# Split weights at a pitch of 130 words per stationary tile, and pairs of activations at multiples of 64 bytes

## The chip, the cores and the metric

The kernel runs on one core of one Trainium2 chip. The metric is the device time of one execution in microseconds (us); three runs of the kernel before took 2317.48 to 2319.41 us, median 2319.04. Five engines work side by side: the tensor engine (PE in the profile; PEld is its loading of stationary operands), the vector engine (DVE), the scalar engine (ACT), GpSimd (POOL), and the sync engine (SP), which issues the loads from DRAM. Matmuls read a stationary operand and a moving one from SBUF, a memory of 128 partitions, and write to PSUM.

## The reference

Three transformer blocks of width 1024 are applied one after the other to 512 tokens, in float32. Nearly all of the arithmetic is products of an activation with a weight matrix; between them stand norms, gates and mixers.

```python
# block 1: adaptive norm; dilated attention and an HGRN2 recurrence; gated sum
proj = h @ w_in[l]
y = sigmoid(g_a) * (o_a @ w_branch_a[l]) + sigmoid(g_b) * (o_b @ w_branch_b[l])
x = x + gate[:, None] * (y @ w_out[l])
...
# block 2: latent attention and a long convolution; a gated feed forward with a short convolution
x = x + y_mix @ w_out[i]
up = _dwconv3(h @ w_up[i], ffn_conv_w[i], ffn_conv_b[i])
x = x + (jax.nn.silu(g) * u) @ w_down[i]
...
# block 3: mLSTM, SSD and retention; a gated feed forward; a last norm
```

## The kernel before

**Products.** Activations lie transposed, with 128 features on the partitions and the 512 tokens along a row. Each operand of these products is split into two float32r parts, a high one and a low one, whose sum is the number. A product of one stationary tile (128 by 128) with one activation tile (128 by 512) is then three matmuls: high weight by high activation, low weight by high activation, high weight by low activation. `acc_T` (line 119) issues them for `nk` tiles in a row into one PSUM bank; eight tiles, 24 matmuls, make one output tile of `proj_T` (line 129). So a new stationary operand is loaded ahead of every matmul.

**Weights.** `raw` (line 95) loads a group of up to 1024 words per partition from DRAM by the sync engine's queue into one of `WRAW` = 4 buffers `wr`. `parts` (line 106) makes the high part `wh` on the scalar engine (line 110, a copy that casts) and the low part `wl` on the vector engine (line 111, a subtraction; four of 370 on GpSimd), in one of `WHL` = 3 buffers each. A buffer of `wh` holds eight stationary tiles end to end, tile k at word 128 k, that is at 512 k bytes. `proj_N` (line 137) uses the same groups the other way round: there an activation tile is stationary and 256 columns of the weights move. The inverse transform of the long convolution (line 1387) and the shared rotary key (line 1241) do so too.

**Activations.** `pair` (line 162) allocates the two parts of an activation tile: `A0` to `A7` live all through, others (`B`, `C`, `a`, `oa`, `ob`, `y` and so on) in pools that open and close with the stages. Where a pair lies depends on what its pool holds before it: the pools stack up, so that a small tile of 160 bytes per partition (`lb`, line 634) or of 16 bytes (`pss`, line 1259) shifts all that is allocated above it.

**Order.** The order of instructions on each engine is settled when the program is built; at run time semaphores alone decide when one may start. A group of weights may be split once the matmuls that read its buffer three groups earlier are done.

Of the kernel before, what the change touches and what calls it, by code (L numbers as in the profile page):

```python
# [25 lines left out]
# ---------------------------------------------------------------- host layout  # L26
def tiles_T(w, ksplit):
    """(K, N) -> for each k split [N/128, 128, nk*128]; lhsT tiles of 128 columns."""
    K, N = w.shape
    a = w.reshape(K // P, P, N // P, P).transpose(2, 1, 0, 3)  # L30
    out, k0 = [], 0
    for nk in ksplit:
        out.append(np.ascontiguousarray(a[:, :, k0 : k0 + nk]).reshape(N // P, P, nk * P))
        k0 += nk
    return out


def tiles_N(w, nk, gc):
    """(K, N) -> [N/gc, K/(128 nk), 128, nk*gc]; moving groups of gc columns."""
    K, N = w.shape  # L40
    a = w.reshape(K // (P * nk), nk, P, N // gc, gc).transpose(3, 0, 2, 1, 4)
    return np.ascontiguousarray(a).reshape(N // gc, K // (P * nk), P, nk * gc)


def cols(v):
    """A vector of n*128 features -> [128, n]."""
    return np.ascontiguousarray(np.asarray(v).reshape(-1, P).T)


def pad_rows(v):  # L50
    """A [k<=128, n] block -> [128, n] with zero rows below."""
    v = np.asarray(v)
    o = np.zeros((P, v.shape[1]), v.dtype)
    o[: v.shape[0]] = v
    return o


class K:
    """The engines, the pools and the operations that all blocks share."""
# [34 lines left out]
    # -------------------------------------------------------------- weights  # L94
# [7 lines left out]
    def w(self, src, n=1024, eng=None):  # L102
        """One group of weights from DRAM, split exactly into two float32r parts."""
        return self.parts(self.raw(src, n), n, eng)

    def parts(self, r, n=1024, eng=None):
        nc = self.nc
        hi = self.wp.tile([P, 1024], F32R, tag="whi", bufs=self.WHL, name=self.name("wh"))
        lo = self.wp.tile([P, 1024], F32R, tag="wlo", bufs=self.WHL, name=self.name("wl"))
        nc.scalar.copy(out=hi[:, :n], in_=r[:, :n])  # L110
        (eng or nc.vector).tensor_tensor(out=lo[:, :n], in0=r[:, :n], in1=hi[:, :n].bitcast(F32), op=ALU.subtract)  # L111
        return hi, lo

    # -------------------------------------------------------------- products
# [3 lines left out]
    def acc_T(self, ps, w, act, nk, start=True, stop=True, m=P, n=T, k0=0):  # L118
        """ps[m, n] += w^T act over nk tiles of 128, three passes each."""
        hi, lo = w  # L120
        for k in range(nk):
            ah, al = act[k0 + k]
            wh, wl = hi[:, k * P : k * P + m], lo[:, k * P : k * P + m]
# [4 lines left out]
    def proj_T(self, srcs, act, tag="mm", bufs=3, nks=(8,), eng=None):  # L128
        """One tile [128 features, 512 tokens] of act @ w; srcs are the k groups."""
# [7 lines left out]
    def proj_N(self, grp, act, nk, gc, evac, tag="mm", bufs=3):  # L137
        """[512 tokens, gc features] of act @ w; grp is [ksplits, 128, nk*gc]."""
# [3 lines left out]
        ws = [self.w(grp[s], nk * gc) for s in range(nks)]  # L142
# [14 lines left out]
    def last_pe(self):  # L157
        """The last instruction of the tensor engine so far."""
        return next(i for i in reversed(self.nc.cur_bb.bb.instructions) if i.engine == mybir.EngineType.PE)

    # -------------------------------------------------------------- pairs
# [3 lines left out]
    def A(self, i):  # L165
        """The i-th of eight pairs that live all through."""
        return self.pair(self.hp, f"A{i}")

    def split(self, pr, src, lo="v", p=P):
        """Two float32r parts of an SBUF tile (or, with lo on the vector engine, a PSUM tile)."""  # L170
# [7 lines left out]
    def split_scaled(self, pr, src, g, p=P):  # L178
        """The parts of src * g with g per partition."""
# [8 lines left out]
    # -------------------------------------------------------------- norms  # L188
    def sq_add(self, acc, i, x, scale=None, tag="sq"):
        """acc (+)= (x * scale)^2 for tile i of a sum; returns acc."""  # L190
# [11 lines left out]
    def col_sums(self, acc, tag="t", bufs=2):  # L202
        """Sums over the partitions of acc [128, 512] (or of several), as [128 tokens, 4]."""
# [13 lines left out]
    def rsqrt(self, src, n, inv, eps=EPS):  # L217
        """(src * inv + eps) ** -0.5 for a small [128, n]."""
# [6 lines left out]
    def rows(self, r, sb=True, tag="t", bufs=2):  # L225
        """r [128 tokens, 4] as rows over all partitions, [128, 512] (in SBUF or PSUM)."""
# [16 lines left out]
class HeadRows:  # L243
    """Factors per token of two heads as rows over 64 partitions each."""

    def __init__(self, k, pool, bufs=1):
        nc = k.nc
        self.k, self.n = k, 0
        # the two parts of the rows (from 0 and from 32), and what spreads them
# [8 lines left out]
    def __call__(self, r, out):  # L258
        """r [128 tokens, 4, 2] -> out [128, 512]."""
# [14 lines left out]
class Norm:  # L274
    """A norm whose factor per token is applied to the products: pairs of x * g are ready tile by tile."""
# [10 lines left out]
    def finish(self):  # L286
        """The pairs; the factor per token follows when it is first used."""
        return self.pairs
# [24 lines left out]
def consts1():  # L313
    v = np.arange(TAB)
    dist = 127 - v + 384  # table entry v holds distance (p - u + 384) with v = u - p + 127
# [48 lines left out]
def rel_table(k, pool):  # L364
    """rel_bias plus the multiplicity of each distance (a last row), as a table in DRAM."""
# [15 lines left out]
def skew_rows(k, s1, s2, pr):  # L381
    """The rows of the table of two heads, once per partition."""
# [3 lines left out]
class Ada:  # L386
    """One third of silu(c) @ w_ada as columns [128, 8], in two halves; with `row`, the second one as a row by the tensor engine."""
# [47 lines left out]
def start(k, early):  # L435
    """x -> the pairs of h, with the work that needs no activations between the loads."""
    nc = k.nc
    with k.tc.tile_pool(name="b1s", bufs=1) as pool:
# [7 lines left out]
        # partly in the places of the pairs of h  # L446
# [53 lines left out]
def attn1(k, h, tab, oa, op):  # L500
    """The merged dilated attention; appends the gated pairs of o_a. Returns the columns of the gate."""
    nc = k.nc
    with k.tc.tile_pool(name="a1", bufs=1) as p:
# [3 lines left out]
        def proj(pr):  # L507
            ps = k.proj_T([k.aps["w1q"][pr]], h)
            # the two parts of a head over each other, k's first part twice
# [119 lines left out]
def bounds(k, p):  # L629
    """What the lower bounds of the forget gates make of tanh."""  # L630
    nc = k.nc
    # lower bound: softmax over the two rows, first of the cumulated
    l0, l1 = k.v("lb0", 0, 8), k.v("lb1", 0, 8)
    lb = p.tile([P, 8, 5], F32, tag="lb", name="lb")
# [8 lines left out]
    # fs = (1 - lb) / 2, fb = lb + fs  # L643
# [3 lines left out]
    # k / 2 = fs / 2 - fs / 2 * tanh  # L647
# [6 lines left out]
def hgrn(k, h, fs, fb, ks, ob, op):  # L654
    """The gated linear recurrence as decayed products inside and between chunks of 128."""
    nc = k.nc
    with k.tc.tile_pool(name="hg", bufs=1) as p:
        lvl = p.tile([P, 576], F32, tag="lvl", name="lvl")
        nc.scalar.dma_start(out=lvl, in_=k.aps["c_lvl"])
        # products inside a chunk, zero above the diagonal  # L660
# [39 lines left out]
        def decays(hd, q, kk, b, v):  # L700
            """The decayed products of all levels, and the states before the chunks."""
            AD = ADs[hd % 2]
            for li, H in enumerate(LV):
# [15 lines left out]
                if li == 0:  # L719
                    # a first half of a chunk and its second half  # L720
# [26 lines left out]
            # between chunks  # L747
# [70 lines left out]
def gate1(k, h, nm, n, s):  # L818
    """A branch gate of a tile."""
# [6 lines left out]
def branch_a(k, h, oa, n, f):  # L826
    """The gated attention branch of a tile."""
# [6 lines left out]
def block1_end(k, h, oa, ob, gate, first, xp, done):  # L834
    """y, the output product and the residual; done(x) is called tile by tile."""
# [25 lines left out]
def block1(k, xp, early, done):  # L861
    """The residual of the first block (before its last norm)."""
    h, tab = start(k, early)
    with k.tc.tile_pool(name="b1", bufs=1) as op:
# [3 lines left out]
        with k.tc.tile_pool(name="b1f", bufs=1) as fp:  # L868
            marks = hgrn(k, h, *lb, ob, op)
            # fill the last head  # L870
# [14 lines left out]
def consts2():  # L885
    f32 = np.float32
    # the even times before the odd ones: frequencies 256 to 511 are the mirror of 0 to 255
    t = np.concatenate([np.arange(0, T, 2), np.arange(1, T, 2)])
    ang = 2 * np.pi * ((2 * np.arange(256)[None, :] + 1) * t[:, None] % 2048) / 2048.0  # [time, freq]
    M = np.stack([np.cos(ang), np.sin(ang)]).reshape(2, NT, P, 2, P)  # part, time tile, time, frequency tile, frequency  # L890
    fw = M.transpose(3, 2, 0, 1, 4)
    inv = M.reshape(2, 2, 256, 2, P).transpose(1, 4, 0, 3, 2) / 512.0  # parity, frequency, part, frequency tile, time
# [10 lines left out]
    rope = np.stack([np.cos(an), np.sin(an)], 1).astype(f32)  # [512, 2, 16]  # L903
# [9 lines left out]
def twice(v):  # L913
    """The rows of v on partitions 0 to 63 and again on 64 to 127."""
# [57 lines left out]
def reduce_angle(k, pool, x, p, tag, n=T, quarter=False):  # L972
    """x modulo 2 pi in [-pi, pi], in place, by three exact parts of 2 pi."""
# [13 lines left out]
class Early2:  # L987
    """What needs no activations: the spectrum of the long filters and the embedding term."""
# [37 lines left out]
    def layer(self, i):  # L1026
        """One layer of the filters: tokens 0 to 255 on partitions 0 to 63, the others on 64 to 127."""
# [15 lines left out]
    def emb(self, ns):  # L1043
        k, p, nc = self.k, self.p, self.k.nc
        for n in ns:
            hi, lo = self.we[n // 4]
            o = n % 4 * 256
# [24 lines left out]
    def spectrum(self, f):  # L1072
        """The sums and differences of the even and the odd times: a frequency and its mirror."""
# [13 lines left out]
def halves(k, w, j, act):  # L1087
    """Part j of 128 frequencies of act, for the even times and for the odd ones."""
    out = []
    for i in range(2):  # L1090
        o = j * 512 + i * 256
# [6 lines left out]
def mirror(k, ps, a, b):  # L1098
    """The sum and the difference of two halves, in a and b."""
# [7 lines left out]
def conv3(k, u, t, ps, bc, w, b, i):  # L1107
    """Centred convolution of 3 taps over the tokens of a product in PSUM, times bc, by u into t."""
# [9 lines left out]
class TwoNorms:  # L1118
    """x1 = rmsnorm(x, g1), and the pairs of x1 * g2 before the factors per token."""
# [42 lines left out]
# the step of the attention after which each tile of the output product of the convolution may run  # L1162
# [8 lines left out]
def mix2(k, h, r12, bc, kf, xp, x1, done):  # L1171
    """Latent attention, the long convolution and their output product."""
    nc = k.nc
    V, G, S = nc.vector, nc.gpsimd, nc.scalar
    with k.tc.tile_pool(name="m2", bufs=1) as p:
# [23 lines left out]
        def rotate(x1, x2, tb, nh):  # L1199
            """Rotation of the halves x1, x2 [128, 4, nh, 16] in place."""  # L1200
# [7 lines left out]
        # the even times before the odd ones, in a tile with the times in turn and in one of two halves  # L1208
# [8 lines left out]
        with k.tc.tile_pool(name="m2a", bufs=1) as pa:  # L1217
            def latent(nm, n, g):
# [11 lines left out]
                # the factor of the norm times the one of h  # L1230
# [9 lines left out]
            # shared rotary key  # L1240
            hi, lo = k.w(k.aps["w2kpe"], 256)
# [17 lines left out]
            pss = p.tile([P, NT], F32, tag="pss", name="pss")  # L1259
# [26 lines left out]
        # heads of q and k  # L1286
        qh = q.rearrange("p t (h e) -> p t h e", h=8)

        def head_sums(x, w, pe, t):
            """The factors of the norms of the heads for the token tile t."""  # L1290
# [1010 lines left out]
```

## Time and profile before

| | |
|---|---|
| three runs | 2317.48, 2319.04, 2319.41 us |
| the profiled execution | span of 2316.4 us from its first to its last instruction (its own time with what lies around the span is not recorded) |
| PE busy | 2267.0 us, 98%, 11180 matmuls |
| DVE, ACT, POOL busy | 1389.2 us (60%), 941.6 us (41%), 537.1 us (23%) |
| DMA | 100 GB/s over the span |
| mean granted clock of PE | 0.989 |

The span is the time on the chip without start and end of the launch. A busy time is the union of an engine's instructions, not their sum: a matmul's record lasts longer than the distance to the next one's start, because consecutive matmuls overlap. So the pace of a stream of matmuls is read from the starts of the first and the last of them and their number, not from the mean duration of one.

### The profile page before, as it was taken

How to read it: one execution, taken by the hardware profiler on the slowest of the kernel's cores; microseconds unless marked ns; L12 is line 12 of the kernel's file. 1: busy time of each engine (PE TensorE's matmuls, PEld its weight loads, DVE VectorE, ACT ScalarE, POOL GpSimd, SP SyncE). 2: the span in 40 equal slices, each digit the busy share in tenths (PEclk: the TensorE clock that was granted, in tenths of full speed). 3: DMA queues.
4: the chain of work that ended last, by engine and by line, in shares of the span. 5: the costliest groups of instructions: out<-in, count | busy, mean ns of one | idle time of the engine just before them, and what ended most of it. 6: DMA issues, size and time to landing. Idle time of an engine off the chain costs nothing.

```text
span 2316.4 us, 29278 instructions
## 1 busy us (share of the span) xinstructions
PE 2267.0 (98%) x11180; PEld 1837.4 (79%) x11180; DVE 1389.2 (60%) x2228; ACT 941.6 (41%) x1579; POOL 537.1 (23%) x457
## 2 busy tenths in 40 slices
PE   7899999999999999999999999999999999999998
PEld 3676798888888985678888887888887888888886
DVE  8754566663354597578637747876757665433333
ACT  4344455552243445644424424444444323322221
POOL 5232445541121135222101103000111211220220
PEclk7999999999999999999999999999999999999999
DMA  8542222124333342123232234212222322223222
GB/s 327 164 145 64 74 65 65 51 66 130 100 95 103 115 140 62 68 93 108 78 123 91 81 126 143 91 65 73 78 92 91 127 73 100 100 79 113 100 81 74
DMA packets 82163, 232.59 MB, mean 100 GB/s; under 512 B 10047, under 2 KB 10943, under 8 KB 82024
## 3 DMA queue, kind: packets, MB, share of 16 engines
q1 hardware_dynamic: 67208, 205.49, 26.9%
q10 hardware_dynamic: 14816, 25.25, 3.4%
q8 instruction: 88, 1.44, 0.2%
q14 instruction: 51, 0.42, 0.1%
HBM read 215.99 MB, written 15.22 MB: 100 GB/s over the span
## 4 chain that ended last, share of the span: by engine, by line
PE 57%; issue 2%; DVE 2%; ACT 1%; DMA 0%; POOL 0%; ACTq 0%; POOLq 0%; DVEq 0%
PE mm L116 48%; PE s L116 3%; PE o L116 3%; PE t L116 1%; PE t L1453 1%; DVE sg L1599 0%; DVE wl L111 0%; PE t L1422 0%; DMA x<-scr_x 0%; DVE x L2267 0%; DVE x L1600 0%; ACT P L1439 0%; ACT wh L110 0%; PE t L1953 0%; ACT A L182 0%
## 5 line engine op out<-in xcount | busy, mean ns | idle before, releaser
L116 PE MATMUL mm<-A,wh 128*128 128x512 f32 (+1 forms) x2192 | 692.6, 392 | 1.0 <-DVE A L183 1.0
L110 ACT CAST wh<-wr 128x1024 fp32r<-128x1024 f32 (+3 forms) x370 | 363.5, 984 | 653.9 <-PE mm L116 463.5
L111 DVE TENSOR_TENSOR wl<-wr,wh 128x1024 fp32r<-128x1024 f32 (+3 forms) x366 | 437.7, 1197 | 296.2 <-ACT wh L110 294.4
L116 PE MATMUL mm<-B,wh 128*128 128x512 f32 x1688 | 541.9, 397 | 3.2 <-DVE B L183 1.9
L116 PEld LDWEIGHTS mm<-A,wh 128*128 128x128 f32 (+1 forms) x2192 | 408.9, 187 | 88.2 <-DVE A L183 1.8
L116 PE MATMUL mm<-A,wl 128*128 128x512 f32 (+1 forms) x1096 | 429.0, 392 | 0.5 <-DVE wl L111 0.5
L116 PEld LDWEIGHTS mm<-B,wh 128*128 128x128 f32 x1688 | 316.4, 188 | 73.9 <-DVE B L183 2.9
L116 PE MATMUL mm<-B,wl 128*128 128x512 f32 x844 | 332.4, 394 | 0.1
L116 PEld LDWEIGHTS mm<-A,wl 128*128 128x128 f32 (+1 forms) x1096 | 205.2, 187 | 43.4 <-DVE wl L111 0.9
L116 PEld LDWEIGHTS mm<-B,wl 128*128 128x128 f32 x844 | 159.0, 188 | 34.5 <-issue 1.5
L116 PE MATMUL mm<-a,wh 128*128 128x512 f32 x448 | 140.4, 389 | 0.0
L222 POOL TENSOR_TENSOR r<-r,mhalf 128x4 f32<-128x4 f32 (+1 forms) x40 | 53.7, 1344 | 350.9 <-DVE r L221 350.9
L239 DVE TENSOR_TENSOR us<-mm,bc 128x512 f32<-128x512 f32 x95 | 65.2, 689 | 99.8 <-PE mm L116 99.0
L175 POOL TENSOR_TENSOR a<-sl,a 128x512 fp32r<-128x512 f32 x28 | 40.5, 1446 | 274.2 <-ACT a L173 274.2
L116 PEld LDWEIGHTS mm<-a,wh 128*128 128x128 f32 x448 | 84.1, 188 | 17.4
L116 PE MATMUL mm<-a,wl 128*128 128x512 f32 x224 | 86.8, 389 | 0.0
L116 PE MATMUL mm<-wh,A 128*128 128x256 f32 x448 | 85.4, 287 | 0.0
L116 PEld LDWEIGHTS mm<-wh,A 128*128 128x128 f32 x448 | 71.6, 193 | 2.4 <-issue 1.0
L2187 POOL TENSOR_TENSOR sl<-sl,bc 128x512 f32<-128x512 f32 x22 | 28.7, 1305 | 167.6 <-DVE sl L1545 167.6
L116 PE MATMUL mm<-wl,A 128*128 128x256 f32 x224 | 64.2, 287 | 1.0 <-DVE wl L111 1.0
L712 ACT ACTIVATE d<-d 128x512 f32<-128x512 f32 x56 | 35.2, 629 | 69.7 <-POOL d L711 69.7
L116 PE MATMUL mm<-wh,B 128*128 128x256 f32 x320 | 61.0, 288 | 0.0
(583 smaller groups left out, 3597.1 us busy)
## 6 DMA issues: line engine op xcount, KB each, us to landing
wr<-w2upg SPq DMA_DIRECT2D x22, 512.0 KB, 3.4
wr<-w2upu SPq DMA_DIRECT2D x22, 512.0 KB, 3.5
wr<-w3fg SPq DMA_DIRECT2D x22, 512.0 KB, 3.4
wr<-w3fu SPq DMA_DIRECT2D x22, 512.0 KB, 3.4
adar<-w1ada SPq DMA_DIRECT2D x32, 256.0 KB, 5.1
wr<-w3out SPq DMA_DIRECT2D x16, 512.0 KB, 3.4
wr<-w2uh SPq DMA_DIRECT2D x12, 512.0 KB, 3.6
wr<-w2dn SPq DMA_DIRECT2D x16, 384.0 KB, 2.9
```

Of the source, the lines that this page charges most:

```text
L110: nc.scalar.copy(out=hi[:, :n], in_=r[:, :n])
L111: (eng or nc.vector).tensor_tensor(out=lo[:, :n], in0=r[:, :n], in1=hi[:, :n].bitcast(F32), op=ALU.subtract)
L116: self.nc.tensor.matmul(out, a, b, start=start, stop=stop)
L175: eng.tensor_tensor(out=l[:p], in0=src, in1=hi[:p].bitcast(F32), op=ALU.subtract)
L222: nc.gpsimd.tensor_tensor(out=r, in0=r, in1=self.mhalf[:, :n], op=ALU.pow)
L239: self.nc.vector.tensor_tensor(out=out, in0=ps, in1=bc, op=ALU.mult)
L712: nc.scalar.activation(out=d, in_=d, func=AF.Exp)
L1453: nc.tensor.transpose(ps[:, i * P : (i + 1) * P], pt[i][:, j * P : (j + 1) * P], k.ident)
L2187: nc.gpsimd.tensor_tensor(out=s, in0=s, in1=norm.bc, op=ALU.mult)
```

## The change

Three things are edited; the rest of the diff takes out comments.

1. A buffer of `wh` or `wl` has 8 × 130 words instead of 1024, and stationary tile k begins at word 130 k (520 k bytes). Its 128 words still lie together; two words between tiles are unused. The cast and the subtraction write it as eight rows of 128 words (128x8x128 in place of 128x1024), and users index it by tile.
2. With `flat=True`, where the weights are the moving operand, a group is laid out end to end as before.
3. `lb` grows from 5 to 6 words per entry (160 to 192 bytes per partition), `pss` from 16 to 64 bytes.

```diff
+    PITCH = 130
-    def parts(self, r, n=1024, eng=None):
+    def parts(self, r, n=1024, eng=None, flat=False):
         nc = self.nc
-        hi = self.wp.tile([P, 1024], F32R, tag="whi", bufs=self.WHL, name=self.name("wh"))
-        lo = self.wp.tile([P, 1024], F32R, tag="wlo", bufs=self.WHL, name=self.name("wl"))
-        nc.scalar.copy(out=hi[:, :n], in_=r[:, :n])
-        (eng or nc.vector).tensor_tensor(out=lo[:, :n], in0=r[:, :n], in1=hi[:, :n].bitcast(F32), op=ALU.subtract)
+        hi = self.wp.tile([P, 8 * self.PITCH], F32R, tag="whi", bufs=self.WHL, name=self.name("wh"))
+        lo = self.wp.tile([P, 8 * self.PITCH], F32R, tag="wlo", bufs=self.WHL, name=self.name("wl"))
+        r = r[:, :n]
+        if flat:
+            hi, lo = hi[:, :n], lo[:, :n]
+        else:
+            hi, lo = (t.rearrange("p (k c) -> p k c", c=self.PITCH)[:, : n // P, :P] for t in (hi, lo))
+            r = r.rearrange("p (k c) -> p k c", c=P)
+        nc.scalar.copy(out=hi, in_=r)
+        (eng or nc.vector).tensor_tensor(out=lo, in0=r, in1=hi.bitcast(F32), op=ALU.subtract)
         return hi, lo
...
     def acc_T(self, ps, w, act, nk, start=True, stop=True, m=P, n=T, k0=0):
         hi, lo = w
         for k in range(nk):
             ah, al = act[k0 + k]
-            wh, wl = hi[:, k * P : k * P + m], lo[:, k * P : k * P + m]
+            wh, wl = hi[:, k, :m], lo[:, k, :m]
...
-        ws = [self.w(grp[s], nk * gc) for s in range(nks)]
+        ws = [self.w(grp[s], nk * gc, flat=True) for s in range(nks)]
...
-    lb = p.tile([P, 8, 5], F32, tag="lb", name="lb")
+    lb = p.tile([P, 8, 6], F32, tag="lb", name="lb")
...
-            pss = p.tile([P, NT], F32, tag="pss", name="pss")
+            pss = p.tile([P, 4 * NT], F32, tag="pss", name="pss")[:, :NT]
```

No engine's instructions change their order: on PE, POOL, ACT, DVE and SP the same instructions stand in the same sequence in the two built programs, 10353 matmuls among them (some of them are several records in the profile). What differs is the form of the 370 casts and subtractions, and where in its partition an operand begins. Counted over the built programs, for the float32r operands of the matmuls, by the start address's remainder modulo 64 bytes:

| operand | matmuls | before | after |
|---|---|---|---|
| stationary `wh`, `wl` (all under moving operands of 512 words) | 7440 | 0 | 0 in 1023; 8, 16, ... 56 in 6417 |
| moving `A`, `C`, `a`, `pa`, most of `B` | 6672 | 0 | 0 |
| moving `y`, `ob`, `oa`, the rest of `B` | 720 | 32 | 0 |
| moving `sm`, `df` | 48 | 32 | 32 |
| moving `wh`, `wl` (256 words) | 1464 | 0 | 0 |
| of these, over stationary `w2cq`, `w2ckv` | 312 | 32 | 0 |
| of these, over stationary `A`, `B` | 1152 | 0 | 0 |
| moving `kT` and stationary `qT` (attention of block 2) | 96 | 0 and 0 | 32 and 32 |
| moving `k`, `kl` and stationary `q` (attention of block 1) | 64 | 32 and 32 | 0 and 0 |

More of the change, by code (lines that the diff above doesn't have):

```diff
@@ L100, with w @@
     WRAW, WHL = 4, 3
-    def w(self, src, n=1024, eng=None):
-        return self.parts(self.raw(src, n), n, eng)
-    def parts(self, r, n=1024, eng=None):
+    PITCH = 130
+    def w(self, src, n=1024, eng=None, flat=False):
+        return self.parts(self.raw(src, n), n, eng, flat)
+    def parts(self, r, n=1024, eng=None, flat=False):
         nc = self.nc
-        hi = self.wp.tile([P, 1024], F32R, tag="whi", bufs=self.WHL, name=self.name("wh"))
-        lo = self.wp.tile([P, 1024], F32R, tag="wlo", bufs=self.WHL, name=self.name("wl"))
-        nc.scalar.copy(out=hi[:, :n], in_=r[:, :n])
-        (eng or nc.vector).tensor_tensor(out=lo[:, :n], in0=r[:, :n], in1=hi[:, :n].bitcast(F32), op=ALU.subtract)
+        hi = self.wp.tile([P, 8 * self.PITCH], F32R, tag="whi", bufs=self.WHL, name=self.name("wh"))
[8 more added lines that the diff above has]
+        (eng or nc.vector).tensor_tensor(out=lo, in0=r, in1=hi.bitcast(F32), op=ALU.subtract)
         return hi, lo
@@ L1046, in emb @@
             hi, lo = self.we[n // 4]
-            o = n % 4 * 256
+            o = n % 4 * 2
             ps = k.bank()
@@ L1090, in halves @@
     for i in range(2):
-        o = j * 512 + i * 256
+        o = j * 4 + i * 2
         ps = k.bank()
@@ L1239, in mix2 @@
             ckv, rkv = latent("w2ckv", 2, "kv_norm")
-            hi, lo = k.w(k.aps["w2kpe"], 256)
+            hi, lo = k.w(k.aps["w2kpe"], 256, flat=True)
             ps = k.bank()
@@ L1386, in inverse @@
                 for i in range(2):
-                    hi, lo = k.w(k.aps["c_inv"][i])
+                    hi, lo = k.w(k.aps["c_inv"][i], flat=True)
                     for j in range(2):
@@ L1503, in out_half @@
                 ps = k.bank(*bank)
-                k.acc_T(ps, tuple(t[:, n % 2 * 512 :] for t in ws[nm]), act, 4)
+                k.acc_T(ps, tuple(t[:, n % 2 * 4 :] for t in ws[nm]), act, 4)
                 return ps
```

## The prediction

> **What bounds the kernel now.** I read the page's busy times first, then the waits of PE, then the chain of work that ended last, then the starts of matmuls in single stretches.
>
> ```profile
> PE 2267.0 (98%) x11180; PEld 1837.4 (79%) x11180; DVE 1389.2 (60%) x2228; ACT 941.6 (41%) x1579; POOL 537.1 (23%) x457
> PE mm L116 <- ACT wh L110: 6.3, 1, 6.3
> PE mm L116 <- DVE wl L111: 1.5, 3, 0.5
> 1053.25 347.71 PE mm L116 x1534
> ```
>
> PE is idle for 2316.4 - 2267.0 = 49.4 us in all. Its waits for weights (columns: total us, times, longest) are 6.3 us once, at the start, and 1.5 us in three pieces. The chain's longest piece (start, length, count) is 1534 matmuls in a row with no wait between them: 347.71 / 1534 = 226.7 ns from one to the next. So the kernel is bound by the pace of its matmuls, and 1 ns on each of the 7440 with a split weight as stationary operand is worth 7.4 us. The change leaves their number and order alone. The question is what an operand's place in memory does to the pace, and the trace of before holds a few places to compare.
>
> ```profile
> 655.28 0.40 PE L116 MATMUL mm<-y,wh 128*128 128x512 f32 x1
> ...
> 699.85 0.40 PE L116 MATMUL mm<-y,wh 128*128 128x512 f32 x1
> L116 PE MATMUL mm<-y,wh x128: 395/395/396, 655.3 to 699.8; 128*128 128x512 f32 x128
> L116 PE MATMUL mm<-y,wl x64: 395/396/396, 655.5 to 699.6; 128*128 128x512 f32 x64
> L116 PE MATMUL mm<-A,wh x352: 389/389/389, 1205.4 to 1324.9; 128*128 128x512 f32 x176
> ```
>
> The pair `y` begins at 32 modulo 64, `A` at 0; stationary weights are at 0 in both. 192 matmuls of `y` give (699.85 - 655.28) / 191 = 233.4 ns, 6.7 ns over the pace above; the single records are longer by the same step (395 against 389 ns, the middle of the three durations).
>
> ```profile
> L116 PE MATMUL mm<-wh,A x64: 278/283/283, 98.0 to 109.4; 128*128 128x256 f32 x64
> L116 PE MATMUL mm<-wl,A x32: 283/283/283, 98.1 to 109.3; 128*128 128x256 f32 x32
> L116 PE MATMUL mm<-wh,w2cq x144: 277/280/283, 766.4 to 791.6; 128*128 128x256 f32 x144
> L116 PE MATMUL mm<-wl,w2cq x72: 277/280/282, 766.5 to 791.5; 128*128 128x256 f32 x72
> 98.00:109.40 11.40, 11.40 (x97) 11.40 (x96) 6.57 (x16) 7.34 (x12) 0.00 (x0) 1.00 0.93 316
> 766.40:791.60 25.20, 25.20 (x217) 25.20 (x217) 5.93 (x8) 9.90 (x19) 0.00 (x0) 1.00 0.39 121
> 1205.30:1324.90 119.60, 119.60 (x530) 99.02 (x529) 85.78 (x107) 50.92 (x64) 12.95 (x10) 1.00 0.28 93
> ```
>
> Here weights are moving, 256 words wide, and activations stationary. Over `A` (at 0) 96 matmuls take (109.4 - 98.0) / 95 = 120.0 ns each; over `w2cq` (at 32) 216 take (791.6 - 766.4) / 215 = 117.2 ns. The windows' third number from the right is the granted clock: 1.00 in all three, so none of this is the clock. Two things follow. First, 512 words cost 226.7 and 256 cost 120.0 ns: 106.7 ns for 256 words, 6.7 ns for 16 words (64 bytes). A moving operand that begins at 32 touches one more piece of 64 bytes, and pays exactly for one more. Secondly, 512 words at that rate are 213.3 ns and 256 are 106.7: **each matmul pays 13.3 ns on top, at both widths**, as much as two pieces of 64 bytes. The stationary operand at 32 is the only row in which that rest is smaller: 117.2 - 106.7 = 10.5 ns. So the rest depends on where the stationary operand begins.
>
> By the Trainium skill, page "TensorE: Matmul & The Clock Gate", section "Back-to-back issue gap", an isolated stream runs at N / 2.4 + 2.5 ns, which would be 215.8 and 109.2 ns; both paces above are 10.9 ns over that. If the whole of this went with the pitch, an estimate from the page would be 6417 x 10.9 = 70 us.
>
> **The change, part by part.** All sums are made against the span of 2316.4 us, which lies 2.6 us below the median of the three runs; I add that at the end.
>
> *Stationary weights off 64 bytes.* 6417 of the 7440 matmuls get a stationary tile at 8, 16, ... 56 modulo 64; every eighth tile stays at 0. No row shows a 512-wide matmul with such a tile. From below, the cost is bounded by the whole rest going: 6417 x 13.3 = 85 us gained. From above, by the slowest steady pace among stretches with both operands at 0, just after a wait:
>
> ```profile
> 826.21 0.40 PE L116 MATMUL mm<-A,wl 128*128 128x512 f32 x1
> 826.44 0.62 PE L116 MATMUL mm<-A,wh 128*128 128x512 f32 x2
> 826.90 0.39 PE L116 MATMUL mm<-A,wl 128*128 128x512 f32 x1
> 827.13 0.62 PE L116 MATMUL mm<-A,wh 128*128 128x512 f32 x2
> 827.60 0.40 PE L116 MATMUL mm<-A,wl 128*128 128x512 f32 x1
> 827.83 0.62 PE L116 MATMUL mm<-A,wh 128*128 128x512 f32 x2
> 828.29 0.39 PE L116 MATMUL mm<-A,wl 128*128 128x512 f32 x1
> ```
>
> Nine matmuls take 828.29 - 826.21 = 2.08 us, 231.1 ns each, before the stream falls into its pace of 226.7. So the same matmuls on the same addresses have a slower, unsettled mode, 4.4 ns longer: 6417 x 4.4 = 28 us lost if the changing start of the stationary tiles kept the stream from settling. I take the row that is nearest, a stationary operand off 64 bytes: 120.0 - 117.2 = 2.8 ns, **6417 x 2.8 = 18.0 us gained**.
>
> *Moving pairs.* 720 matmuls of `y`, `ob`, `oa` and some of `B` go from 32 to 0: **720 x 6.7 = 4.8 us gained**, well shown by the rows above. Part of those of `B` run in stretches that wait for other engines, so 4 to 4.8 us.
>
> *What the same shifts make worse.* `kT` goes from 0 to 32: 96 x 6.7 = 0.6 us lost at most. `w2cq` and `w2ckv` go from 32 to 0 as stationary operands, where they had the better pace: 312 x 2.8 = 0.9 us lost. `k` and `kl` of block 1 gain (64 matmuls, under 0.5 us, left out).
>
> *Padded writes.* The 370 casts and subtractions write eight rows of 512 bytes instead of one of 4096.
>
> ```profile
> L110 ACT CAST wh<-wr 128x1024 fp32r<-128x1024 f32 x287 | 300.7, 1050 | 473.2 <-PE mm L116 313.6 <-issue 139.6 <-PE s L116 13.8
> L111 DVE TENSOR_TENSOR wl<-wr,wh 128x1024 fp32r<-128x1024 f32 x283 | 366.2, 1295 | 182.7 <-ACT wh L110 181.3
> L111 POOL TENSOR_TENSOR wl<-wr,wh x4: 2378/2406/2798, 14.2 to 809.4; 128x1024 fp32r<-128x1024 f32 x4
> ```
>
> A cast takes 1.05 us and a subtraction 1.30 us for a group that feeds 24 matmuls, 24 x 226.7 = 5.44 us, and the casts mostly wait for PE to free a buffer (313.6 us of idle time). That lead of up to three groups covers them. I take no cost; the lower end is also nothing, as they move the same words. For the upper end I let the subtraction take as long as GpSimd's, 2.4 us: DVE would be busy 1389 + 370 x 1.1 = 1796 us, 78%, and PE's waits for weights (6.3 + 1.5 us) might double, 8 us. The order on all engines is the same, and no DMA changes.
>
> **The sum:** -18.0 - 4.8 + 0.6 + 0.9 = -21.3 us, nearly all of it on the path, as PE waits for hardly anything: a span of 2295.1, and 2297.7 us beside the median. After a gain on PE, what is late next is nothing at this size: ACT and DVE have over a third of their time free.
>
> **The rivals.**
>
> *The rest mostly goes.* If the rest comes from both operands changing their 64 bytes at the same moments, a start of 8 or 24 may do more than the 32 that I have a row for, as 32 is itself a half of the piece. Half of the rest, one piece of 6.7 ns, is 6417 x 6.7 = 43 us: with the other terms -46, 2273 us. For it: the rest is the same at 256 and 512 words, so it hangs on the load of the stationary operand. Against: at 32 only a fifth of it went.
>
> *The pitch does nothing.* What remains is -4.8 + 0.6 + 0.9 = -3.3 us, 2315.7 us. For it: the difference of 2.8 ns is from one stage, with moving operands half as wide, where loads of stationary operands fill the whole time (PEld 25.20 of 25.20 us, against 99.02 of 119.60). The Trainium skill, page "SBUF — State Buffer", section "Who interferes with whom", says that PE has two independent read ports, for moving and stationary operands, and never waits on anyone; by that rule this rival would hold, and the difference between `A` and `w2cq` speaks against it.
>
> *Slower: the stream no longer settles.* The pace of 226.7 comes only after some ten matmuls with equal starts. If eight starts in turn keep it in the mode of 231.1 ns, the loss is 28.2 - 3.3 = 24.9 us, 2344 us. It decides from the first stage on and would show in the long stretches from 1053 and 1970 us, where before nothing disturbs the stream. For it: the slow mode exists at unchanged addresses. Against: over `w2cq`, which never settles into one distance either (277 to 283 ns), the mean is better, not worse.
>
> **How the numbers follow.** Forecast -21.3 us (2297.7; its own range 2280 to 2312): 0.42. Rest mostly gone: 0.18. Pitch does nothing: 0.16. Slower: 0.24, padded writes that cost included. The range leaves out about 6 in 100 below (more than two thirds of the rest gone, 2258) and about 10 above (the slower case beyond its price): 2258 to 2344. About 0.2%, 4.6 us, is what a measurement of this kernel can tell from no change; the case of no effect lies within that, so faster 0.60, same 0.16, slower 0.24.
>
> **What would show it.** The chain's long stretch should be at 224 ns a matmul instead of 226.7 (220 in the first rival, 226.7 in the second, 231 in the third); `y` at the pace of `A`, not 6.7 ns over it; `w2cq` near 120 ns; casts and subtractions at 1.05 and 1.30 us. I am wrong if the pace of the 512-wide stream does not move with the stationary tile's start, or moves the other way.

## The result, and the profile after

The changed kernel takes 2345.8 us (2343.66 to 2346.83, four runs), the kernel before 2319.22 us (2317.48 to 2325.0, four runs). The ratio is 1.0113, with a 95% interval of 1.0098 to 1.0128: slower by 1.1%, 26.6 us. The forecast was a gain of 21 us; the time lies outside the range, and beside the price of the third rival (2344).

The profile after, first the busy times of the page:

```profile
PE 2296.9 (98%) x11180; PEld 1839.8 (78%) x11180; DVE 1385.7 (59%) x2228; ACT 941.6 (40%) x1579; POOL 538.4 (23%) x457
```

PE's waits for weights (total us, times, longest):

```profile
PE mm L126 <- ACT wh L120: 5.9, 1, 5.9
PE mm L126 <- DVE wl L121: 1.2, 4, 0.5
```

The two longest pieces of the chain that ended last (start, length, count):

```profile
1058.08 355.78 PE mm L126 x1534
1990.30 308.86 PE mm L126 x1332
```

The casts and subtractions, in the groups of instructions (busy us, mean ns, idle time before them):

```profile
L120 ACT CAST wh<-wr 128x1024 fp32r<-128x1024 f32 x287 | 300.6, 1049 | 490.6 <-PE mm L126 328.2 <-issue 144.8 <-PE s L126 14.1
L121 DVE TENSOR_TENSOR wl<-wr,wh 128x1024 fp32r<-128x1024 f32 x283 | 365.1, 1291 | 186.7 <-ACT wh L120 185.0 <-issue 0.8
```

PE is busy 29.9 us longer, and its idle time (2344.4 - 2296.9 = 47.5 us) did not grow. The same 1534 matmuls in a row, with no wait between them, take 355.78 us instead of 347.71: 231.9 ns each, where they took 226.7. So the loss is the pace of the matmuls. Casts and subtractions take what they took (1049 and 1291 ns), and PE waits no longer for them.

Here are `y` and `w2cq`, by tile (durations in ns least, middle, most; first and last start):

```profile
L126 PE MATMUL mm<-y,wh x128: 387/394/401, 658.8 to 703.1; 128*128 128x512 f32 x128
L126 PE MATMUL mm<-wh,w2cq x144: 274/280/283, 770.6 to 795.9; 128*128 128x256 f32 x144
```

A piece of the long stretch in order of time (start, length):

```profile
1085.98 0.39 PE L126 MATMUL mm<-A,wl 128*128 128x512 f32 x1
1086.21 0.63 PE L126 MATMUL mm<-A,wh 128*128 128x512 f32 x2
1086.68 0.39 PE L126 MATMUL mm<-A,wl 128*128 128x512 f32 x1
1086.91 0.64 PE L126 MATMUL mm<-A,wh 128*128 128x512 f32 x2
1087.38 0.39 PE L126 MATMUL mm<-A,wl 128*128 128x512 f32 x1
```

The durations of `y` now spread over 387 to 401 ns, where they were 395 or 396. From one start to the next there are now 226 to 240 ns, where there were 231 to 235. Six matmuls of `A` take 1087.38 - 1085.98 = 1.40 us, 233 ns each. Added up over the single starts of the whole trace, the distances from one matmul 512 words wide to the next of that width grew by 30.1 us (1779.4 to 1809.5), and those between neighbours 256 words wide shrank by 2.4 us (188.6 to 186.2): 27.7 us, against 28.0 us between the spans.

### The profile page after: what moved, and what is told of

Same layout as the page of the kernel before. It is cut to its first block, busy times and chain, and to the rows that moved or that the text cites. A ratio compares the mean times of both kernels' runs of the same rounds, so it can differ in the third digit from the quotient of the medians.

```text
span 2344.4 us, 29278 instructions
## 1 busy us (share of the span) xinstructions
PE 2296.9 (98%) x11180; PEld 1839.8 (78%) x11180; DVE 1385.7 (59%) x2228; ACT 941.6 (40%) x1579; POOL 538.4 (23%) x457
## 4 chain that ended last, share of the span: by engine, by line
PE 58%; issue 2%; DVE 1%; ACT 1%; DMA 0%; POOL 0%; ACTq 0%; POOLq 0%; DVEq 0%
PE mm L126 49%; PE s L126 3%; PE o L126 3%; PE t L126 1%; PE t L1465 1%; DVE sg L1611 0%; DVE wl L121 0%; DMA x<-scr_x 0%; PE t L1434 0%; DVE x L2279 0%; DVE x L1612 0%; ACT P L1451 0%; ACT wh L120 0%; PE t L1965 0%; ACT A L192 0%
## 5 line engine op out<-in xcount | busy, mean ns | idle before, releaser
L126 PE MATMUL mm<-A,wh 128*128 128x512 f32 (+1 forms) x2192 | 703.6, 397 | 0.9 <-DVE A L193 0.9
L126 PE MATMUL mm<-B,wh 128*128 128x512 f32 x1688 | 549.2, 401 | 3.1 <-DVE B L193 1.9
L1586 DVE TENSOR_TENSOR x<-x,mm 128x512 f32<-128x512 f32 x32 | 22.0, 688 | 67.3 <-PE mm L126 67.3
```

Of the source, the lines that this page charges most:

```text
L126: self.nc.tensor.matmul(out, a, b, start=start, stop=stop)
L1586: k.nc.vector.tensor_tensor(out=xs[n], in0=xs[n], in1=ps, op=ALU.add)
```

## The experiments

Three theories stood at the start: A, stationary tiles that begin at changing places within 64 bytes keep the stream from settling; B, any start off 64 bytes costs; C, the buffers of 4160 bytes, which shift everything behind them by multiples of 64 bytes, do it. "Distance" below is the stationary tile's start minus the moving tile's, modulo 256 bytes, counted over the built programs.

**The padding of `lb` and `pss` alone.**

```diff
-    lb = p.tile([P, 8, 5], F32, tag="lb", name="lb")
+    lb = p.tile([P, 8, 6], F32, tag="lb", name="lb")
...
-            pss = p.tile([P, NT], F32, tag="pss", name="pss")
+            pss = p.tile([P, 4 * NT], F32, tag="pss", name="pss")[:, :NT]
```

> The kernel before with lb and pss padded alone; the weights stay at a pitch of 128 words. All theories on the pitch agree here: the 720 matmuls whose moving pairs go from 32 to 0 modulo 64 bytes should gain 6.7 ns each (y at 226.7 ns, as A), 96 with kT and 312 over w2cq and w2ckv lose 0.6 and 0.9 us: 3.3 us less than before, about 2316 us.

Measured: 2316.14 us (11 runs) beside 2319.67; ratio 0.9984, 0.9975 to 0.9993. In the trace of this kernel, `y` by tile:

```profile
L116 PE MATMUL mm<-y,wh x128: 389/389/389, 653.2 to 696.5; 128*128 128x512 f32 x128
```

Five rows of `B` in order of time:

```profile
1007.84 0.40 PE L116 MATMUL mm<-B,wl 128*128 128x512 f32 x1
1008.07 0.64 PE L116 MATMUL mm<-B,wh 128*128 128x512 f32 x2
1008.54 0.39 PE L116 MATMUL mm<-B,wl 128*128 128x512 f32 x1
1008.77 0.62 PE L116 MATMUL mm<-B,wh 128*128 128x512 f32 x2
1009.23 0.39 PE L116 MATMUL mm<-B,wl 128*128 128x512 f32 x1
```

The total is as expected, and `y` has 43.3 us / 191 = 226.7 ns. But the 240 matmuls of `B` that went from 32 to 0 modulo 64 as well still take (1009.23 - 1007.84) / 6 = 232 ns, hardly less than the 233 they took before. No theory had forecast that. `y`, `ob` and `oa` went from a distance of 32 to 0, these `B` from 160 to 128.

**More room between the weight buffers, and a common offset.** Tiles at a pitch of 128 words; `lb` and `pss` as before. The diff is against the changed kernel and shows room; off32 has 8 in place of the 0.

```diff
-    PITCH = 130
+    PITCH, WORDS, OFF = 128, 1040, 0
...
-        hi = self.wp.tile([P, 8 * self.PITCH], F32R, tag="whi", bufs=self.WHL, name=self.name("wh"))
+        hi = self.wp.tile([P, self.WORDS], F32R, tag="whi", bufs=self.WHL, name=self.name("wh"))
...
-            hi, lo = (t.rearrange("p (k c) -> p k c", c=self.PITCH)[:, : n // P, :P] for t in (hi, lo))
+            hi, lo = (t[:, self.OFF : self.OFF + 8 * self.PITCH].rearrange("p (k c) -> p k c", c=self.PITCH)[:, : n // P, :P] for t in (hi, lo))
```

> The kernel before with weight buffers of 1040 words (4160 bytes) in place of 1024, tiles still at a pitch of 128 words, lb and pss as before. It shifts the buffers against each other and against the activations by multiples of 64 bytes, as the change does, and nothing else. Theory A (the loss comes from stationary tiles that begin at changing places within 64 bytes) and theory B (it comes from any start off 64 bytes, one more piece to fetch): no change, 2319 us, long stretches at 226.7 ns. Theory C (it comes from where the buffers lie against each other in multiples of 64 bytes): about 2345 us, 231.9 ns.

> As room, but every stationary tile begins 8 words (32 bytes) later, at a pitch of 128 words, so all at 32 modulo 64; weights that move stay at 0. Theory A: the start is the same for all tiles, so the stream settles: 226.7 ns or, by the row over w2cq, 224 ns; 2298 to 2319 us. Theory B: every tile is off 64 bytes, at least 231.9 ns in the long stretches, 2347 us or more. Theory C: as room.

Measured: room 2340.34 us, ratio 1.009 (1.0075 to 1.0106); off32 2342.48 us, ratio 1.0097 (1.0084 to 1.0111). The longest pieces of the two chains, room first:

```profile
1051.78 354.94 PE mm L126 x1534
```

```profile
1054.34 355.24 PE mm L126 x1534
```

That is 231.4 and 231.6 ns. Room has every stationary tile at 0 modulo 64 and no change of place within 64 bytes, and shows most of the loss, 4.7 of 5.2 ns in the long stretch and about 21 of 27 us in all: A and B fall as its only cause, and C holds in its numbers. Off32 gives every stationary tile the same start modulo 64, for which A had forecast 2298 to 2319 us. In room the distances of `A`, `B`, `C` and `a` are 0, 64, 128 and 192 in turn as the buffers rotate.

**Streams of matmuls alone.** 96 matmuls for each of 34 layouts, run once, in the kernel's order of three per tile, high and low buffers and activations all starting at the same place modulo 512 bytes.

```python
for k in range(NK):
    a = slice(so + k * sp, so + k * sp + c)
    m = slice(mo + k * T, mo + k * T + w)
    nc.tensor.matmul(ps[:c, :w], hi[:, a], ah[:, m], start=k == 0, stop=False)
    nc.tensor.matmul(ps[:c, :w], lo[:, a], ah[:, m], start=False, stop=False)
    nc.tensor.matmul(ps[:c, :w], hi[:, a], al[:, m], start=False, stop=k == NK - 1)
```

> Only streams of matmuls, 96 for each of 34 layouts, in the kernel's order of three matmuls per tile; the reference is not computed, the output is the product of the last layout, copied. Stationary tiles at a constant offset (codes s.), moving tiles at an offset (m.), both (b.), pitches of 129 to 256 words (p.), narrower moving operands (w.) and fewer stationary columns (c.). All: base and again at 226.7 ns. Theory A: constant offsets of 2 to 14 words keep 226.7 ns or less, pitches 130 and 132 give about 232 ns, pitches 144 and 160 (all tiles at 0 modulo 64) 226.7. Theory B: every offset or pitch that isn't a multiple of 16 words is at 231 ns or more. Theory C: offsets of 16, 32, 48 words and pitches of 144 and 160 also give about 232 ns. If the rest of 13.3 ns hangs on the stationary operand's load, 64 columns should have about half of it, 220 ns.

The instructions of this kernel by tile (durations least, middle, most; first and last start; from the first to the last of these 32 there are 93 distances):

```profile
L79 PE MATMUL sh<-ah,hi x32: 395/396/396, 107.3 to 129.0; 128*128 128x512 f32 x32
L79 PE MATMUL sp<-ah,hi x32: 393/396/398, 196.9 to 218.6; 128*128 128x512 f32 x32
L79 PE MATMUL ss<-ah,hi x32: 389/389/389, 263.5 to 284.6; 128*128 128x512 f32 x32
L79 PE MATMUL mq<-ah,hi x32: 390/393/404, 351.9 to 373.5; 128*128 128x512 f32 x32
L79 PE MATMUL mr<-ah,hi x32: 389/389/393, 374.2 to 395.3; 128*128 128x512 f32 x32
L79 PE MATMUL bh<-ah,hi x32: 387/389/393, 418.1 to 439.2; 128*128 128x512 f32 x32
L79 PE MATMUL pb<-ah,hi x32: 392/394/397, 462.2 to 483.8; 128*128 128x512 f32 x32
L79 PE MATMUL pp<-ah,hi x32: 389/397/398, 529.0 to 550.5; 128*128 128x512 f32 x32
L79 PE MATMUL cb<-ah,hi x32: 390/392/397, 690.4 to 711.9; 128*32 128x512 f32 x32
```

The starts are given to 0.1 us, so that a pace worked out from them is good to about 1 ns. Stationary tiles 32 bytes on (sh): 21.7 / 93 = 233.3 ns. 64 bytes on (sp): 233.3. 256 bytes on (ss): 21.1 / 93 = 226.9. Moving tiles 128 bytes on (mq): 232.3; 256 bytes on (mr): 226.9. **Both 32 bytes on (bh): 226.9, although no tile is then at 0 modulo 64.** A pitch of 130 words (pb) gives 232.3 with no buffer shifted, and one of 144 words (pp, all tiles at 0 modulo 64) 231.2. By the single starts in the trace, with the settled end of each stream alone (the last 60 distances), 256-byte steps and bh are at 226.67, pp at 231.7, and the moving tile 64 bytes on (mp) at 228.9. The seven constant offsets of 8 to 56 bytes (sb to sn) lie at 230.0 to 233.3, against theory A, and pp speaks against both A and B. Loads of 64 or 32 stationary columns (cd, cb) did not halve the rest but left the stream at 230 to 232 ns: at a distance of 0 the rest does not shrink with the load.

From this came theory D: what counts is the distance modulo 256 bytes; at 0 the stream settles at 226.7 ns, elsewhere it runs at 229 to 234.

**Theory D in the whole kernel: shift all activations.** The weight buffers stay as they are. The diff is against the kernel before and shows pad64; pad192 and pad256 have 48 and 64 words.

```diff
+        nc.gpsimd.memset(self.hp.tile([P, 16], F32, tag="pad", name="pad"), 0.0)
```

> The kernel before with 64 unused bytes between the weight buffers and the activations: all moving tiles shift by 64 bytes, the weight buffers lie as before and every start stays at its remainder modulo 64. Theory D (the pace hangs on the distance between the stationary and the moving tile modulo 256 bytes; equal is the settled pace of 226.7 ns): 6660 matmuls get the distance of -64 bytes, which the stream mp showed at 228.9 ns, 2.2 ns more: 14.8 us, about 2334 us. Theory C2 (the distance between the high and the low weight buffers): no change, 2319 us. The reading of the prediction (only the remainder modulo 64 of each tile counts): no change.

> As pad64 with 192 bytes. Theory D: the distance is +64 bytes for 6660 matmuls, which the stream sp showed at 233.3 ns, 6.7 ns more: 44 us, about 2364 us. Theory C2 and the reading of the prediction: no change, 2319 us.

> As pad64 with 256 bytes. Theory D: no distance changes modulo 256, so 2319 us and 226.7 ns in the long stretches, as before. If what counts is the distance modulo 512 bytes or more, or any shift, slower, as pad64.

Measured: pad64 2326.74 us (ratio 1.0034, 1.0021 to 1.0047), pad192 2352.73 us (1.0141, 1.0126 to 1.0156), pad256 2319.38 us (0.9997, 0.9987 to 1.0006). The longest pieces of the three chains, in this order:

```profile
1053.43 351.12 PE mm L117 x1534
```

```profile
1059.63 357.93 PE mm L117 x1534
```

```profile
1053.55 347.71 PE mm L117 x1534
```

228.9, 233.3 and 226.7 ns: the paces that the streams showed for these distances, to the tenth. The other two readings predicted no difference between the three. The totals are 7 and 11 us under the sums, for two reasons that the traces show. Not all matmuls at a distance of 0 ran at the settled pace before: over all of `A` in the kernel before, waits left out, the mean is 227.4 ns, slow stretches like the one after a wait in the prediction included, and it rose to 229.2 and 233.3, by less than 2.2 and 6.7. So the 512-wide distances grew by 12.2 us in pad64, not 14.8 (35.9 in pad192, not 44). And the products with moving weights, whose distance left 0 as well, got faster: 3.9 us in pad64, 3.6 in pad192.

**More layouts as streams.** The same kernel with separate offsets for high and low parts.

> Streams as in bench1, for other layouts; the reference is not computed, the output is the last layout's product, copied. Codes r.: both weight parts at 1, 24, 40 to 63 words; h.: only the low weights shifted, a.: only the low activations; b.: all four shifted alike by 2, 16, 32, 28 words; n.: 508 to 480 moving words; f.: 256 moving words over shifted stationary tiles; c.: 96 stationary columns. Theory D: base, again, bp and bq at 226.7 ns, all r. between 228 and 234, h. and a. between 226.7 and 234 as a third or more of their pairs are out of step; none below 226.7. The f. codes are open: 117 to 120 ns.

```profile
L86 PE MATMUL rn<-ah,hi x32: 389/389/389, 285.8 to 306.9; 128*128 128x512 f32 x32
L86 PE MATMUL hq<-ah,hi x32: 387/396/398, 352.2 to 373.7; 128*128 128x512 f32 x32
L86 PE MATMUL bb<-ah,hi x32: 389/392/393, 485.3 to 506.7; 128*128 128x512 f32 x32
L86 PE MATMUL nd<-ah,hi x32: 378/378/378, 638.3 to 658.4; 128*128 128x480 f32 x32
L86 PE MATMUL fa<-ah,hi x32: 277/280/285, 659.1 to 670.1; 128*128 128x256 f32 x32
L86 PE MATMUL fb<-ah,hi x32: 281/281/282, 670.4 to 681.4; 128*128 128x256 f32 x32
L86 PE MATMUL fd<-ah,hi x32: 285/285/285, 693.0 to 704.2; 128*128 128x256 f32 x32
```

The paces here are those of the single starts, over the last 60 distances. Low weights 128 bytes on alone (hq) bring the whole stream to 231.1 ns: one tile in three is enough. Both weight parts shifted (r.) lie at 228.3 to 234.3 ns, as expected within 0.3 ns, but for a miss: a distance of -4 bytes (rn, 63 words) settles at 226.67. Another: both tiles 8 bytes on (bb) or 112 bytes on (br) run at 231.1 in spite of a distance of 0; so did both 16 bytes on in the first set (bd, 230.0), while 32, 64 and 128 bytes (bh, bp, bq) settle. Nothing at 512 words ran below 226.67.

At 256 moving words a distance of 0 is among the slow places: 120.0 ns at 0, and the same at 128 (fd) and 160 bytes, against 118.3 at 32 bytes (fa), 117.8 at 64 (fb), and 117.3 to 117.8 at 96, 192 and 224. The width counts too. 480 words (nd) take 216.7 ns and 496 take 223.3, which is 6.7 ns for 16 words once more; but at the prediction's rate of 106.7 ns for 256 words, each of these matmuls pays 16.7 ns beyond its words, where 256, 512 and (in the first set) 384 words pay 13.3.

**The last tiles in step.** `pss` takes 192 bytes, so that all of `B` gets a distance of 0.

```diff
-            pss = p.tile([P, 4 * NT], F32, tag="pss", name="pss")[:, :NT]
+            pss = p.tile([P, 12 * NT], F32, tag="pss", name="pss")[:, :NT]
```

> As align, with pss at 192 instead of 64 bytes, so that the last 240 matmuls over B, and w2cq and w2ckv, too stand at a distance of 0 modulo 256 bytes. Theory D: those of B go from about 232 to 227 ns (1.2 us, some of it in stretches that wait for other engines), the 312 over w2cq and w2ckv to 120 ns (0.3 us lost): about 1 us less than align, 4 us less than before, 2315 to 2316 us beside 2319 to 2320. The reading of the prediction (remainder modulo 64 of each tile): as align.

Measured: 2315.5 us (11 runs) beside 2319.66; ratio 0.9986, 0.9977 to 0.9995. The starts of `B` in its trace:

```profile
1008.05 0.39 PE L116 MATMUL mm<-B,wl 128*128 128x512 f32 x1
1008.28 0.62 PE L116 MATMUL mm<-B,wh 128*128 128x512 f32 x2
1008.73 0.39 PE L116 MATMUL mm<-B,wl 128*128 128x512 f32 x1
1008.96 0.62 PE L116 MATMUL mm<-B,wh 128*128 128x512 f32 x2
1009.41 0.39 PE L116 MATMUL mm<-B,wl 128*128 128x512 f32 x1
```

1.36 us for six, 226.7 ns, as expected. `w2cq`, now at a distance of 0 as a stationary operand, slowed down to (792.1 - 766.3) / 215 = 120.0 ns, as expected too:

```profile
L116 PE MATMUL mm<-wh,w2cq x144: 283/283/283, 766.3 to 792.1; 128*128 128x256 f32 x144
```

What this run adds to align is under what the runs can tell. Both beat the kernel before by about 4 us, and the changed one by 30.

## Why the prediction was wrong

**What bounds the kernel: right.** PE's pace is the time, 1 ns on each matmul is 7 us, and the change is seen nowhere else.

**The reading of the rows: where it went wrong first.** From `y` at 32 modulo 64 and `A` at 0, I wrote that a moving operand that begins at 32 touches one more piece of 64 bytes and pays for one more. The step of 6.7 ns is real, and its agreement with the price of 16 words is exact, but the cause is another: in the stream bh both operands begin at 32 and none of it is paid, while in pad192 6660 matmuls have both operands at 0 modulo 64 and pay 6.7 ns. In the kernel before, all activations but a few lay at 0 from the weights modulo 256 bytes, and `y`, `ob`, `oa` and a part of `B` did not. I compared each tile with multiples of 64 and never the two operands with each other, though the built programs held both starts.

**Stationary weights off 64 bytes: the step that failed, with the wrong sign.** The largest term of the sum, -18.0 us, was 2.8 ns gained on each of 6417 matmuls, from the row over `w2cq`. The runs showed a loss in its place: 5.2 ns a matmul in the long stretch (231.9 against 226.7). That row is right (117.2 ns at a distance of 96 bytes, and the streams of that width over shifted tiles give 117.3 to 120.0), but it is 256 words wide, and there a distance of 0 is among the slow places; at 512 words it is the fast one. The row was nearest in the stationary tile's address and far in the width. In the changed kernel only 232 of 7440 matmuls with split stationary weights have a distance of 0, where 6660 had it before, and the stream does not settle: 30.1 us lost on matmuls 512 words wide.

**Moving pairs: right in the sum, by luck in a part.** -3.3 us in all was forecast for padding alone, -3.5 measured. But the 240 matmuls of `B` gained next to nothing from a start at 0 modulo 64 and needed a distance of 0; the term was 480 x 6.7 = 3.2 us, not 4.8. What was set against it did not come in full: in align `w2cq` lost 1.3 ns, not 2.8, and the matmuls with `kT` nothing. In the changed kernel even that gain goes, as `y` is at (703.1 - 658.8) / 191 = 232 ns.

**Padded writes: right.** No cost.

**`w2cq` and `w2ckv`: wrong.** About 120 ns was forecast; `w2cq` is at (795.9 - 770.6) / 215 = 117.7. The 120 come at a distance of 0, as in align2; in the changed kernel the moving weights' buffers shifted too, and only 72 of the 216 have it.

**The rivals.** The third, the stream that no longer settles, had the price right (231.1 against 231.9 ns, 2344 against 2345.8 us), from a row of the trace in which a slow mode stood. Why that row, at a distance of 0 just after a wait, has the pace of a mixture of distances, no run shows; the agreement is in part luck. Its mechanism was only partly right: eight starts in turn are enough (pb, 232.3 ns), but so is one constant distance other than 0 (pad192, sh), and the room between buffers alone (231.4). I gave it 0.24, because over `w2cq` an unsettled stream was the faster one. The second, by the Trainium skill's page "SBUF — State Buffer", section "Who interferes with whom", had PE's two read ports independent. The traces disagree with what that made of the time: at the same addresses modulo 64 the pace goes from 226.7 to 233.3 ns with the distance between the two operands alone. Whether it is at the read ports that the two meet, no run shows. That the rest of 13.3 ns might mostly go did not happen in any layout: 226.67 ns was the least of all streams 512 words wide. Nor did any come near 215.8 ns, the estimate from N / 2.4 + 2.5 ns of the Trainium skill's page "TensorE: Matmul & The Clock Gate", section "Back-to-back issue gap".

## What to carry to other kernels

Compare the pace of matmuls by the place of the stationary and the moving operand to each other, not of each by itself; here 256-byte steps between them kept the fast pace, and weight buffers that grew by 64 bytes each cost 0.9% (room). A padding that shifts what is allocated behind it is a change of its own, to be tried with the padding alone. Where a row from another shape is the only one at hand, its sign is no safer than its size.

## What was not expected of the hardware

- The pace of a stream of 128x512 float32r matmuls, each with a load of its own, is 226.67 ns when both operands begin at the same place modulo 256 bytes (and at a multiple of 32; both shifted by 8, 16 or 112 bytes run at 230.0 to 231.1), and 228 to 234 ns at nearly all other distances tried; +64 bytes cost 6.7 ns, -64 bytes 2.2 ns, -4 bytes nothing. At 256 moving words the in-step layout is one of the slow ones, 120.0 against 117.3 to 118.3 ns at most others.
- One of three matmuls out of step is enough to slow the stream: 231.1 ns with the low weights alone 128 bytes on.
- Loading fewer stationary columns did not shorten the time from one matmul to the next: 230 to 232 ns with 96, 64 or 32 columns where both operands begin at the same place. At a distance of 64 bytes it did, from 233.3 with 128 columns to 228.3 with 96.
- Why 256 bytes, and what the 13.3 ns are that a matmul of 256, 384 or 512 words pays beyond its words (16.7 at 480 and 496), stays open.
